# Gated delta rule in a two-layer decoder: the keys' scale in three instructions of VectorE instead of five of GpSimd, the queries' scale in two of GpSimd instead of five

## The chip, the cores and the metric

The kernel is one program on one core of a Trainium2 chip. The metric is the device time of one execution in microseconds (us). On the core, TensorE multiplies matrices into PSUM, VectorE (DVE in the profile) and ScalarE (ACT) work on elements, GpSimd (POOL) works on elements in SBUF, and SyncE (SP) issues most of the loads. Each engine runs its own instructions in order; they wait for each other by semaphores.

## The reference

Two decoder layers run over a prompt of 256 tokens and over 8 sequences of 4 sample tokens. The first layer's mixer is retention, the second's the gated delta rule; after each stands a gated ConvFFN. The change lies in the delta rule. What matters of it, cut:

```python
q = jnp.repeat(l2norm(q), rep, axis=2) * GDN_DK ** -0.5     # rep = 2 value heads for a key head
k = jnp.repeat(l2norm(k), rep, axis=2)
beta = jax.nn.sigmoid(b)
...
kb = kc * bc[..., None]                                      # keys times beta
L = jnp.where(tri_strict, jnp.einsum('bhid,bhjd->bhij', kb, kc) * decay, 0.0)
sol = lax.linalg.triangular_solve(eye + L, rhs, ...)         # (I + L)^-1
u, w = sol[..., :dv], sol[..., dv:]
v_new = u - w @ S
attn = jnp.einsum('bhid,bhjd->bhij', qc, kc) * decay
o = (qc * exp(G)) @ S + attn @ v_new
...
o = o * rsqrt(mean(o * o) + EPS) * norm_w * silu(z)
```

## The kernel before, in words

Activations are kept transposed: features on the 128 partitions, 288 columns of tokens (256 prompt, 32 sample). A projection is made by `product` (L527): for each output tile of 128 features 24 matmuls of 128 by 288, 8 for each of three pairs of high and low parts (`whi` with `hh`, `whi` with `hl`, `wlo` with `hh`), each weight block being split into `whi` by ScalarE (L416) and `wlo` by VectorE (L417) as it comes in.

The delta rule has 16 value heads in four groups of four heads (g is 0 to 3; two key heads in a group). `GDN_ORDER` (L34) gives the order of the projections: K is keys and queries (`gk`), V is values (`gv`), Z is the gate (`gz`), D is the output projection (`down`). Everything else is written as generators that are advanced every six matmuls, and so lies between the projections' matmuls. For each group:

- `gdn_norms` (L1157) sums the squares of keys and queries (tile `kss`, the last part by the small matmuls `pq`), takes the reciprocal root by nine small VectorE instructions (`rsqrt`, L541; the result is `krs`, its last instruction L557), and makes the keys' scale: `ksc[:,1]` is beta times the reciprocal norm squared, for two halves of the prompt (jt) and four heads; `ksc[:,0]` is its negative. This is where the first half of the change lies (L1190 to L1195).
- `gdn_scores` (L1275) multiplies keys by keys and queries (`pa`, 512 columns, and `pb`) for the group's two key heads, j is 0 and 1, and VectorE turns each pair into `gnn` and `gat` (L1291 to L1296: six instructions and two). `pa` and `pb` of the second key head take the PSUM banks of the first (`PA_TAGS`, L59), so they wait until its `gat` has been made.
- `gdn_inverse` (L1299) inverts I + L: first the 32 by 32 diagonal blocks by a chain of VectorE instructions (`mp`, `Ti`, L1332 to L1338, three a step), then a round trip through DRAM (`ud`, then `uc`, L1344 and L1346, both on SP's queue, which also carries the weights' loads `raw`), then small matmuls `pe` (L1358). The inverse of group g runs beside the norms of group g+1.
- `gdn_samples` (L1438) does the sample tokens (`psy`, `pso`); `gdn_heads` (L1562) and `gdn_finish` (L1607) solve, make the output, and update the state (`gpS`, L1636). `gdn_finish` makes the queries' scale `qs` (reciprocal norm times 1/sqrt(128), for eight columns of the prompt and one of the samples): the second half of the change (L1617 to L1622).

The program is handed to a scheduler which works out the order of each engine's instructions as the program is built. An engine's order is thus not always that of the code, and changes when instructions are changed.

Of the kernel before, what the change touches and what calls it, by code (L numbers as in the profile page):

```python
# [10 lines left out]
ALU = mybir.AluOpType  # L11
# [3 lines left out]
P = 128  # L15
# [280 lines left out]
class Program:  # L296
# [860 lines left out]
    def gdn_norms(self, g, d):  # L1157

        nc, gp = self.nc, self.gp
        t = lambda tag, shape, dt=F32, bufs=1: gp.tile(shape, dt, tag=tag, name=f"{tag}_{g}", bufs=bufs)  # L1160
        kqT, kt = d["kqT"], d["kt"]

        ss = t("kss", [P, 10], bufs=2)
        for j in range(2):
            yield from self.lag(d, ("kq", 0, j), CONV_STEPS)
            pt = self.aux(f"pk{g}{j}", "a")
            for i in range(2):
                nc.tensor.transpose(pt[:, i * P : (i + 1) * P], kqT[:, j, 0, i * P : (i + 1) * P], self.ident)
            for i in range(2):
                nc.scalar.activation(t("junk", [P, P], bufs=2), pt[:, i * P : (i + 1) * P], AF.Square, accum_out=ss[:, 2 * i + j : 2 * i + j + 1])  # L1170
            nc.scalar.copy(kt[:, :, j, :], pt[:, 0:TP].rearrange("p (i d) -> p i d", d=P))
        for j in range(2):
            yield from self.lag(d, ("kq", 1, j), CONV_STEPS)
            if j == 0:
                pq = self.aux(f"pq{g}", "a")
            for i in range(2):
                nc.tensor.matmul(pq[:, 2 * i + j : 2 * i + j + 1], lhsT=d["sq", j][:, i * P : (i + 1) * P], rhs=self.ones[:, 0:1], start=True, stop=True)
        while "sqd" not in d or self.nexg is None:
            yield
        for s in range(2):  # L1180
            nc.tensor.matmul(pq[:, 4 + s : 5 + s], lhsT=d["sqd"][:, s, :], rhs=self.ones[:, 0:1], start=True, stop=True)
        nc.vector.tensor_copy(ss[:, 4:10], pq[:, 0:6])
        nc.vector.tensor_scalar(ss, ss, EPS, None, ALU.add)
        rr = t("krs", [P, 10], bufs=2)
        self.rsqrt(rr, ss, 1.0, 0.0, f"k{g}")
        nm = t("knm", [P, 10], bufs=2)
        nc.vector.tensor_tensor(nm, ss, rr, ALU.mult)

        sc = t("ksc", [P, 3, 2, 4], bufs=2)
        for jt in range(2):  # L1190
            for j in range(2):
                bsl = self.beta[:, jt, 4 * g + 2 * j : 4 * g + 2 * j + 2]
                c = 2 * jt + j
                nc.gpsimd.tensor_scalar(sc[:, 1, jt, 2 * j : 2 * j + 2], bsl, rr[:, c : c + 1], rr[:, c : c + 1], ALU.mult, ALU.mult)
        nc.gpsimd.tensor_scalar(sc[:, 0], sc[:, 1], -1.0, None, ALU.mult)  # L1195
        d.update(sc=sc, rr=rr, nm=nm)

    def gdn_scores_all(self, ds):
# [408 lines left out]
    def gdn_finish(self, g, a):  # L1607

        nc, gp, A = self.nc, self.gp, self.A
        t = lambda tag, shape, dt=F32, bufs=1: gp.tile(shape, dt, tag=tag, name=f"{tag}_{g}", bufs=bufs)  # L1610
        big = lambda sh, dt=F32: self.big(sh, dt, "c", 512, BIG_C, 1)
        h4 = lambda v: v.rearrange("p (h d) -> p h d", d=P)
        kt, sc, rr, ss, osm, u, pos = (a[k] for k in ("kt", "sc", "rr", "ss", "osm", "u", "pos"))
# [2 lines left out]

        qs = t("qs", [P, 9], bufs=1)  # L1617
        f = float(P) ** -0.5
        for it in range(2):
            for j in range(2):  # L1620
                nc.gpsimd.tensor_scalar(qs[:, 4 * it + 2 * j : 4 * it + 2 * j + 2], self.ones[:, 0:2], rr[:, 4 + 2 * it + j : 5 + 2 * it + j], f, ALU.mult, ALU.mult)
        nc.gpsimd.tensor_scalar(qs[:, 8:9], rr[:, 9:10], f, None, ALU.mult)  # L1622
        s2 = t("oss2", [P, 9])
        nc.vector.tensor_tensor(s2, ss, qs, ALU.mult)
# [118 lines left out]
```

## Time and profile before

| | us |
|---|---|
| median of 3 runs | 1236.23 |
| lowest and highest | 1225.26, 1239.33 |
| the profiled execution's own time | 1233.65 |
| its span, from the first to the last instruction | 1231.9 |

TensorE is busy for 95% of the span, VectorE for 71%, ScalarE for 49%, GpSimd for 27%. TensorE's mean granted clock is 0.972 of full speed (2.4 GHz); where it isn't full it is half (1.2 GHz). The delta rule's part of the span reaches from about 600 to 960 us. An engine's idle time has a cost where TensorE, which is nearly always busy, is made to wait in the end. In the rows, a name in brackets says how long the engine had been idle before the instruction and what ended the wait.

### The profile page before, as it was taken

How to read it: one execution, taken by the hardware profiler on the slowest of the kernel's cores; microseconds unless marked ns; L12 is line 12 of the kernel's file. 1: busy time of each engine (PE TensorE's matmuls, PEld its weight loads, DVE VectorE, ACT ScalarE, POOL GpSimd, SP SyncE). 2: the span in 40 equal slices, each digit the busy share in tenths (PEclk: the TensorE clock that was granted, in tenths of full speed). 3: DMA queues.
4: the chain of work that ended last, by engine and by line, in shares of the span. 5: the costliest groups of instructions: out<-in, count | busy, mean ns of one | idle time of the engine just before them, and what ended most of it. 6: DMA issues, size and time to landing. Idle time of an engine off the chain costs nothing.

```text
span 1231.9 us, 24934 instructions
## 1 busy us (share of the span) xinstructions
PE 1164.1 (95%) x9486; PEld 1049.1 (85%) x9486; DVE 870.3 (71%) x2003; ACT 608.8 (49%) x1256; POOL 327.7 (27%) x507
## 2 busy tenths in 40 slices
PE   6999999999999999999989998988899899999996
PEld 2879798797969999997777788977889699999996
DVE  3657574765766666667679888797965588777775
ACT  2444534344445544444674645744544365555553
POOL 0213142251302122222252223233222113223232
PEclk9999999999999999999999988988989899999998
DMA  9998696877699556557636641533434897777621
GB/s 365 345 332 324 227 336 233 313 246 242 211 314 393 189 171 190 171 181 259 209 92 211 223 144 63 159 129 115 131 103 129 298 357 239 258 254 253 196 76 56
DMA packets 97480, 269.08 MB, mean 218 GB/s; under 512 B 26816, under 2 KB 29088, under 8 KB 97232
## 3 DMA queue, kind: packets, MB, share of 16 engines
q1 hardware_dynamic: 87456, 234.57, 57.2%
q0 software_dynamic: 8032, 29.16, 6.3%
q10 hardware_dynamic: 1872, 3.76, 0.8%
q8 instruction: 75, 1.23, 0.4%
q14 instruction: 45, 0.37, 0.1%
HBM read 236.06 MB, written 31.39 MB: 217 GB/s over the span
## 4 chain that ended last, share of the span: by engine, by line
PE 78%; DVE 12%; DMA 3%; ACT 3%; issue 2%; POOL 1%; SPq 0%; POOLq 0%; ACTq 0%; DVEq 0%
PE down L535 17%; PE fg L535 12%; PE fv L535 12%; PE pg L535 4%; PE pv L535 4%; PE adaP L455 4%; PE p L535 3%; PE gv L535 2%; PE gz L535 2%; DVE wlo L417 2%; DVE mp L1332 2%; PE gk L535 2%; PE pO L898 1%; PE pU L917 1%; PE pS L868 1%
## 5 line engine op out<-in xcount | busy, mean ns | idle before, releaser
L417 DVE TENSOR_TENSOR wlo<-more,whi 128x1024 fp32r<-128x1024 f32 x138 | 171.1, 1241 | 74.5 <-ACT whi L416 63.2
L416 ACT CAST whi<-more 128x1024 fp32r<-128x1024 f32 x138 | 144.3, 1047 | 136.5 <-PE down L535 53.1
L417 DVE TENSOR_TENSOR wlo<-raw,whi 128x1024 fp32r<-128x1024 f32 x123 | 155.4, 1267 | 70.6 <-ACT whi L416 48.4
L416 ACT CAST whi<-raw 128x1024 fp32r<-128x1024 f32 x123 | 128.1, 1044 | 133.5 <-PE down L535 32.8
L716 POOL TENSOR_TENSOR x<-x,dt 128x32 f32<-128x32 f32 x159 | 100.6, 634 | 135.2 <-DVE dt L714 134.1
L712 DVE SCALAR_TENSOR_TENSOR x<-down,mod,x 128x256 f32<-128x256 f32 x160 | 76.6, 479 | 51.3 <-PE down L535 50.5
L591 POOL TENSOR_TENSOR fal<-cv,fah 128x288 fp32r<-128x288 f32 x44 | 41.6, 945 | 215.7 <-ACT fah L590 180.7
L535 PE MATMUL down<-fal,whi 128*128 128x288 f32 x352 | 64.0, 294 | 0.0
L535 PE MATMUL down<-fah,whi 128*128 128x288 f32 x352 | 62.3, 294 | 0.0
L535 PE MATMUL down<-fah,wlo 128*128 128x288 f32 x352 | 62.1, 294 | 0.0
L535 PE MATMUL fg<-hh_ffn,whi 128*128 128x288 f32 x352 | 58.9, 300 | 1.2 <-ACT hh_ffn L637 1.2
L918 DVE SCALAR_TENSOR_TENSOR S<-S,pU 128x512 f32<-128x512 f32 x64 | 42.2, 684 | 24.2 <-PE pU L917 24.1
L535 PE MATMUL fv<-hh_ffn,whi 128*128 128x288 f32 x352 | 58.7, 298 | 0.0
L535 PEld LDWEIGHTS fg<-hh_ffn,whi 128*128 128x128 f32 x352 | 50.6, 189 | 5.6 <-ACT hh_ffn L646 2.6
L535 PE MATMUL fg<-hh_ffn,wlo 128*128 128x288 f32 x352 | 55.0, 296 | 0.0
L535 PE MATMUL fv<-hh_ffn,wlo 128*128 128x288 f32 x352 | 54.8, 295 | 0.0
L535 PE MATMUL fv<-hl_ffn,whi 128*128 128x288 f32 x352 | 54.3, 295 | 0.0
L535 PE MATMUL fg<-hl_ffn,whi 128*128 128x288 f32 x352 | 54.0, 295 | 0.0
L535 PEld LDWEIGHTS fv<-hh_ffn,whi 128*128 128x128 f32 x352 | 50.5, 189 | 2.5 <-ACT ftail L947 1.2
L535 PEld LDWEIGHTS down<-fah,whi 128*128 128x128 f32 x352 | 51.8, 188 | 0.8 <-ACT whi L416 0.4
L535 PEld LDWEIGHTS down<-fal,whi 128*128 128x128 f32 x352 | 52.3, 188 | 0.2 <-issue 0.2
L535 PEld LDWEIGHTS down<-fah,wlo 128*128 128x128 f32 x352 | 52.0, 188 | 0.0
(492 smaller groups left out, 2923.4 us busy)
## 6 DMA issues: line engine op xcount, KB each, us to landing
raw<-in_wada SPq DMA_DIRECT2D x69, 512.0 KB, 4.9
more<-in_wu SPq DMA_DIRECT2D x68, 512.0 KB, 4.9
raw<-in_wgi SPq DMA_DIRECT2D x48, 512.0 KB, 3.9
more<-in_wada SPq DMA_DIRECT2D x43, 512.0 KB, 5.9
more<-in_wd SPq DMA_DIRECT2D x41, 512.0 KB, 4.4
S<-in_sr SPq DMA_DIRECT2D x16, 1024.0 KB, 8.0
out_rs<-S POOLq DMA_DIRECT2D x16, 1024.0 KB, 8.1
raw<-in_wri SPq DMA_DIRECT2D x28, 512.0 KB, 4.9
```

Source lines behind the costliest of these rows:

```text
L416: nc.scalar.copy(hi[:, :c], r)
L417: nc.vector.tensor_tensor(lo[:, :c], r, hi[:, :c].bitcast(F32), ALU.subtract)
L455: nc.tensor.matmul(self.adaP[32 * g : 32 * g + 32, 0:256], lhsT=self.cs[:, k, :], rhs=rv[:, :, g, :], start=(k == 0), stop=(k == KT - 1), ...
L535: self.nc.tensor.matmul(out, lhsT=av[:, k, c0 : c0 + m], rhs=b[:, k, :], start=(k0 == 0 and i == 0), stop=(k1 == kts and i == len(seq) - 1))
L591: (nc.gpsimd if pool_lo else nc.vector).tensor_tensor(lo, src, hi.bitcast(F32), ALU.subtract)
L712: nc.vector.scalar_tensor_tensor(xm[:, :TP], p[:, :TP], g[:, 0:1], xm[:, :TP], ALU.mult, ALU.add)
L716: (nc.vector if gate == 11 and last and m == KT - 1 else nc.gpsimd).tensor_tensor(xv, xv, t, ALU.add)
L868: nc.tensor.matmul(pS, lhsT=kt[:, j, c * P : (c + 1) * P], rhs=vt[:, j, :], start=(j == 0), stop=(j == 1))
L898: nc.tensor.matmul(pO4[32 * g : 32 * g + 32, :], lhsT=qm[:, c, 4 * bb + g, :], rhs=S[bb, c][:, g, :], start=(bb == 0 and c == 0), stop=Fal ...
L917: nc.tensor.matmul(pU, lhsT=kms[g][:, c * P : (c + 1) * P], rhs=vst, start=True, stop=True)
L918: nc.vector.scalar_tensor_tensor(S[bb, c][:, g, :], S[bb, c][:, g, :], gamma4, pU, ALU.mult, ALU.add)
L1332: nc.vector.tensor_tensor(m, Ti[:, 0:k, :].rearrange("p j c -> p c j").unsqueeze(1).to_broadcast([P, w, 8, k]), X[:, 0:k, i:k].rearrange(" ...
```

## The change

The keys' scale: GpSimd made it by four instructions of 128 by 2 and one negation of 128 by 8. Now VectorE squares the four reciprocal norms into a new tile `kr2` (shown as `kr_0` to `kr_3` in the order), multiplies beta by it in one instruction whose second operand is repeated for the two heads, and negates the result. The queries' scale: four GpSimd instructions of 128 by 2 become one of 128 by 8; the fifth, for the samples, stays.

```diff
@@ gdn_norms
         sc = t("ksc", [P, 3, 2, 4], bufs=2)
-        for jt in range(2):
-            for j in range(2):
-                bsl = self.beta[:, jt, 4 * g + 2 * j : 4 * g + 2 * j + 2]
-                c = 2 * jt + j
-                nc.gpsimd.tensor_scalar(sc[:, 1, jt, 2 * j : 2 * j + 2], bsl, rr[:, c : c + 1], rr[:, c : c + 1], ALU.mult, ALU.mult)
-        nc.gpsimd.tensor_scalar(sc[:, 0], sc[:, 1], -1.0, None, ALU.mult)
+        r2 = t("kr2", [P, 4], bufs=2)
+        nc.vector.tensor_tensor(r2, rr[:, 0:4], rr[:, 0:4], ALU.mult)
+        by_h = lambda v: v.rearrange("p t (j h) -> p t j h", h=2)
+        nc.vector.tensor_tensor(
+            by_h(sc[:, 1]), by_h(self.beta[:, 0:2, 4 * g : 4 * g + 4]),
+            r2.rearrange("p (t j) -> p t j", j=2).unsqueeze(3).to_broadcast([P, 2, 2, 2]), ALU.mult
+        )
+        nc.vector.tensor_scalar(sc[:, 0], sc[:, 1], -1.0, None, ALU.mult)
         d.update(sc=sc, rr=rr, nm=nm)
@@ gdn_finish
-        for it in range(2):
-            for j in range(2):
-                nc.gpsimd.tensor_scalar(qs[:, 4 * it + 2 * j : 4 * it + 2 * j + 2], self.ones[:, 0:2], rr[:, 4 + 2 * it + j : 5 + 2 * it + j], f, ALU.mult, ALU.mult)
+        nc.gpsimd.tensor_scalar(qs[:, 0:8].rearrange("p (c h) -> p c h", h=2), rr[:, 4:8].unsqueeze(2).to_broadcast([P, 4, 2]), f, None, ALU.mult)
         nc.gpsimd.tensor_scalar(qs[:, 8:9], rr[:, 9:10], f, None, ALU.mult)
```

The number of matmuls, loads and ScalarE instructions is the same; GpSimd has 32 instructions fewer, VectorE 12 more. Up to the first group's scale all engines keep their order. Behind it the order moves in many places; three of them follow. The lines of the changed kernel are two higher from L1197 on.

VectorE at the first group's scale, before (`ssc` is the samples' scale):

```order
L557 SCALAR_TENSOR_TENSOR krs_7197<-rsu_k_7199,krs_7197 128x10
L1187 TENSOR_TENSOR knm_7209<-kss_6914,krs_7197 128x10
L1455 TENSOR_SCALAR ssc_7571<-bs,krs_7197 128x1
L1456 TENSOR_SCALAR ssc_7571<-ssc_7571 128x1
L1457 TENSOR_SCALAR ssc_7571<-ssc_7571,exs 128x1
L1291 SCALAR_TENSOR_TENSOR gnn_7225<-pa_7263,ksc_7211,gat_6973 128x128
```

The same place in the changed kernel:

```order
L557 SCALAR_TENSOR_TENSOR krs_7197<-rsu_k_7199,krs_7197 128x10
L1187 TENSOR_TENSOR knm_7209<-kss_6914,krs_7197 128x10
L1191 TENSOR_TENSOR kr_0_7212<-krs_7197 128x4
L1457 TENSOR_SCALAR ssc_7570<-bs,krs_7197 128x1
L1193 TENSOR_TENSOR ksc_7211<-beta,kr_0_7212 128x8
L1458 TENSOR_SCALAR ssc_7570<-ssc_7570 128x1
L1459 TENSOR_SCALAR ssc_7570<-ssc_7570,exs 128x1
L1197 TENSOR_SCALAR ksc_7211<-ksc_7211 128x8
L1293 SCALAR_TENSOR_TENSOR gnn_7224<-pa_7262,ksc_7211,gat_6973 128x128
```

The three new instructions stand between the samples' scale and the first `gnn`; TensorE's order is the same as before here.

VectorE at the second group's scale, before (`mp` and `Ti` belong to the first group's inverse):

```order
L557 SCALAR_TENSOR_TENSOR krs_7867<-rsu_k_7869,krs_7867 128x10
L1332 TENSOR_TENSOR mp_7389<-Ti_7332,X_7331 128x16x31
L1187 TENSOR_TENSOR knm_7879<-kss_7503,krs_7867 128x10
L1291 SCALAR_TENSOR_TENSOR gnn_7893<-pa_7933,ksc_7881,gat_7174 128x128
L1292 SCALAR_TENSOR_TENSOR gnn_7893<-pa_7933,gat_7174 128x128
```

The same place in the changed kernel:

```order
L557 SCALAR_TENSOR_TENSOR krs_7866<-rsu_k_7868,krs_7866 128x10
L1334 TENSOR_TENSOR mp_7388<-Ti_7331,X_7330 128x16x31
L1187 TENSOR_TENSOR knm_7878<-kss_7502,krs_7866 128x10
L1191 TENSOR_TENSOR kr_1_7881<-krs_7866 128x4
L1338 TENSOR_REDUCE Ti_7331<-mp_7388 128x16
L1193 TENSOR_TENSOR ksc_7880<-beta,kr_1_7881 128x8
L1340 SCALAR_TENSOR_TENSOR Ti_7331<-Ti_7331,xp_7338 128x8
L1197 TENSOR_SCALAR ksc_7880<-ksc_7880 128x8
L1334 TENSOR_TENSOR mp_7388<-Ti_7331,X_7330 128x256
L1293 SCALAR_TENSOR_TENSOR gnn_7891<-pa_7931,ksc_7880,gat_7174 128x128
```

Three instructions of the inverse have moved from behind the scores to ahead of them, between the new ones.

TensorE at the second group's second key head, before:

```order
L1493 MATMUL psy_7842<-t_0_7776,t_0_7592 128x128
L464 MATMUL adaT<-cst,adaev 128x128 x2
L1288 MATMUL pa_7967<-kqT_7484 128x512
L1493 MATMUL psy_7896<-t_0_7844,t_0_7592 128x128
L1289 MATMUL pb_7968<-kqT_7484 128x256
L535 MATMUL gz_8076<-hh_gdn,whi 128x288 x6
```

The same place in the changed kernel:

```order
L1495 MATMUL psy_7841<-t_0_7775,t_0_7591 128x128
L464 MATMUL adaT<-cst,adaev 128x128 x2
L1495 MATMUL psy_7894<-t_0_7843,t_0_7591 128x128
L535 MATMUL gz_8074<-hh_gdn,whi 128x288 x8
L535 MATMUL gz_8074<-hl_gdn,whi 128x288 x2
L1290 MATMUL pa_7965<-kqT_7483 128x512
```

Ten matmuls of the gate's projection have moved ahead of `pa`. In the third group seven have moved in the same way (twelve stand ahead of `pa` where five did), and on VectorE one `mp` and one `Ti` have moved ahead of the scores.

TensorE at the fourth group's second key head, before (`down` is the third group's output projection, of 96 matmuls; `pe` belongs to the third group's inverse):

```order
L535 MATMUL down<-gah_8870,whi 128x288 x4
L535 MATMUL down<-gal_8871,whi 128x288 x4
L535 MATMUL down<-gah_8870,wlo 128x288 x4
L1288 MATMUL pa_10053<-kqT_9421 128x512
L1289 MATMUL pb_10054<-kqT_9421 128x256
L1358 MATMUL pe_10121<-uc_10078,gnn_8993 32x32 x16
L535 MATMUL gv_10226<-hh_gdn,whi 128x288 x4
```

The same place in the changed kernel:

```order
L1290 MATMUL pa_10043<-kqT_9415 128x512
L1291 MATMUL pb_10044<-kqT_9415 128x256
L1360 MATMUL pe_10111<-uc_10068,gnn_8987 32x32 x16
L535 MATMUL down<-gah_8865,whi 128x288 x4
L535 MATMUL down<-gal_8866,whi 128x288 x4
L535 MATMUL down<-gah_8865,wlo 128x288 x4
```

Before, all 96 of `down` stood ahead of `pa`; now 72 do, and 24 stand behind the first `pe`. On VectorE the last `Ti` of the third group's inverse now stands only seven instructions ahead of this group's first `gnn`.

SP's queue at the same place, before:

```order
L1344 DMA ud_10073<-t1k_10071 32x256 x4
L402 DMA raw<-in_wgi 128x1024 x2
L1346 DMA uc_10078<-ud_10073 128x8x32
L1317 DMA Ti_10286<-in_unit 128x256
L402 DMA raw<-in_wgi 128x1024
```

The same place in the changed kernel:

```order
L1346 DMA ud_10063<-t1k_10061 32x256 x4
L1319 DMA Ti_10276<-in_unit 128x256
L1348 DMA uc_10068<-ud_10063 128x8x32
L402 DMA raw<-in_wgi 128x1024 x3
```

The way back from DRAM (`uc`) now stands ahead of the two weight loads that it stood behind.

## Rows read from the trace of the kernel before

**Rows 1.** The page: the span, and the engines' busy time with its share of the span and their instructions.

```profile
span 1231.9 us, 24934 instructions
PE 1164.1 (95%) x9486; PEld 1049.1 (85%) x9486; DVE 870.3 (71%) x2003; ACT 608.8 (49%) x1256; POOL 327.7 (27%) x507
```

**Rows 2.** The waits of TensorE from 580 to 960 us, what it was to issue and what it waited for: us in total, times, the longest.

```profile
PE pa L1288 <- DVE gat L1295: 7.3, 4, 2.2
PE gpS L1636 <- DVE bigc L1631: 5.8, 3, 4.3
...
PE psy L1493 <- ACT t L1488: 2.6, 2, 2.4
```

**Rows 3.** The tiles of the keys' scale and of the queries' scale: the instructions that write them, with the shortest, median and longest duration in ns, and the first and last start.

```profile
L1194 POOL TENSOR_SCALAR ksc<-beta,krs x16: 327/335/1374, 624.2 to 841.7; 128x2 f32<-128x2 f32 x16
L1195 POOL TENSOR_SCALAR ksc<-ksc x4: 242/250/252, 627.2 to 842.1; 128x8 f32<-128x8 f32 x4
L1621 POOL TENSOR_SCALAR qs<-ones,krs x16: 258/268/977, 625.6 to 894.1; 128x2 f32<-128x2 f32 x16
```

**Rows 4.** The timeline at the first group's scale: start, duration, engine, line, instruction; in brackets the idle time before it and what ended it.

```profile
622.98 1.05 POOL L1245 TENSOR_TENSOR decay<-cst_g,ghl 128x512 fp32r<-128x512 f32 x1 [1.38 <-PE pd L1262]
623.16 0.90 DVE L557 SCALAR_TENSOR_TENSOR krs<-rsu_k,krs 128x10 f32<-128x10 f32 x1
624.10 0.17 DVE L1187 TENSOR_TENSOR knm<-kss,krs 128x10 f32<-128x10 f32 x1
...
627.24 0.25 POOL L1195 TENSOR_SCALAR ksc<-ksc 128x8 f32<-128x8 f32 x1
627.40 0.55 PE L535 MATMUL gv<-hl_gdn,whi 128*128 128x288 f32 x3
...
627.53 0.35 DVE L1291 SCALAR_TENSOR_TENSOR gnn<-pa,ksc,gat 128x128 f32<-128x128 f32 x1 [2.77 <-POOL ksc L1195]
...
628.97 0.68 DVE L1295 TENSOR_TENSOR gat<-pa,gat 128x512 f32<-128x512 f32 x1
...
629.70 0.70 PE L1288 MATMUL pa<-kqT 128*128 128x512 f32 x1 [1.75 <-DVE gat L1295]
```

**Rows 5.** The timeline at the second group's scale.

```profile
678.04 0.16 DVE L557 SCALAR_TENSOR_TENSOR krs<-rsu_k,krs 128x10 f32<-128x10 f32 x1
678.16 1.14 DVE L1332 TENSOR_TENSOR mp<-Ti,X 128x496 f32<-128x496 f32 x1
...
680.85 0.35 DVE L1291 SCALAR_TENSOR_TENSOR gnn<-pa,ksc,gat 128x128 f32<-128x128 f32 x1 [1.47 <-POOL ksc L1195]
681.10 0.38 PE L464 MATMUL adaT<-cst,adaev 128*128 128x128 f32 x2
...
683.02 1.13 PE L1288 MATMUL pa<-kqT 128*128 128x512 f32 x2 [1.54 <-DVE gat L1295]
...
683.42 0.66 DVE L1336 TENSOR_REDUCE Ti<-mp 128x16 f32<-128x496 f32 x1
```

**Rows 6.** The timeline at the third group's scale.

```profile
760.47 0.16 DVE L557 SCALAR_TENSOR_TENSOR krs<-rsu_k,krs 128x10 f32<-128x10 f32 x1
...
762.06 0.82 PE L535 MATMUL gz<-hh_gdn,whi 128*128 128x288 f32 x5
...
762.45 0.35 DVE L1291 SCALAR_TENSOR_TENSOR gnn<-pa,ksc,gat 128x128 f32<-128x128 f32 x1 [1.38 <-POOL ksc L1195]
...
764.72 1.10 PE L1288 MATMUL pa<-kqT 128*128 128x512 f32 x2 [1.84 <-DVE gat L1295]
764.82 0.62 DVE L1332 TENSOR_TENSOR mp<-Ti,X 128x256 f32<-128x256 f32 x1
```

**Rows 7.** The timeline at the fourth group's scale (SPq is SP's queue).

```profile
834.56 0.41 DVE L1336 TENSOR_REDUCE Ti<-mp 128x8 f32<-128x256 f32 x1
...
838.50 2.77 SPq L402 DMA_DIRECT2D raw<-in_wgi  x2
...
841.48 1.26 SPq L1346 DMA_DIRECT2D uc<-ud  x1
...
842.37 0.35 DVE L1291 SCALAR_TENSOR_TENSOR gnn<-pa,ksc,gat 128x128 f32<-128x128 f32 x1 [1.47 <-POOL ksc L1195]
...
844.54 1.33 PE L1288 MATMUL pa<-kqT 128*128 128x512 f32 x2 [2.19 <-DVE gat L1295]
...
846.21 1.22 PE L1289 MATMUL pb<-kqT 128*128 128x256 f32 x2 [0.34 <-DVE gat L1296]
846.32 0.83 POOL L1353 COPY TT<-uc 32x256 f32<-32x256 f32 x2 [3.78 <-DMA uc<-ud]
...
849.60 0.63 PE L1358 MATMUL pe<-uc,gnn 32*32 32x32 f32 x15 [2.18 <-DVE uc L1347]
```

**Rows 8.** The engines' busy time in stretches of the span: us, then busy time (and instructions) of PE, PEld, DVE, ACT, POOL, then TensorE's granted clock, the DMA share and GB/s.

```profile
844.00:848.00 4.00, 2.55 (x4) 0.80 (x4) 3.40 (x10) 0.85 (x3) 0.79 (x2) 0.67 0.36 88
848.00:852.00 4.00, 2.40 (x45) 2.06 (x47) 3.82 (x11) 1.13 (x3) 1.81 (x3) 0.50 0.00 0
852.00:856.00 4.00, 4.00 (x64) 3.74 (x61) 1.66 (x6) 1.97 (x5) 1.22 (x4) 0.55 0.38 137
```

**Rows 9.** The same view, for a stretch between a scale and the next state update, and for the stretch of that update.

```profile
700.00:720.00 20.00, 19.82 (x259) 18.20 (x258) 13.26 (x36) 16.99 (x57) 5.90 (x16) 1.00 0.57 153
720.00:740.00 20.00, 17.02 (x172) 14.64 (x172) 19.22 (x60) 6.32 (x22) 6.72 (x12) 0.83 0.48 157
```

## The prediction

> **What bounds the kernel now.** I read the page first: TensorE is busy for 1164 of 1232 us [rows 1], so a change is worth what it gives TensorE to do earlier, and not what it takes from VectorE or GpSimd. Then TensorE's waits in the delta rule's part [rows 2]: the longest in total, 7.3 us in four waits, is `pa` waiting for `gat`, once a group. Who is late there is in the timeline of each of the four places. In each, the last instruction of `krs` ends, GpSimd makes `ksc`, VectorE stands idle for 1.38 to 2.77 us until GpSimd's negation (L1195) is done, then makes six `gnn` and one `gat`, and TensorE issues `pa` within 0.1 us of that `gat`'s end, after an idle time of 1.75, 1.54, 1.84 and 2.19 us [rows 4 to 7]. So the keys' scale lies on the path that ends last, four times, and the sum is made of these four places. From the first `gnn` to the end of `gat` takes 2.12 us (627.53 to 629.65), of which the six `gnn` take 0.24 us each [rows 4].
>
> The sum is made against the profiled execution: 1233.65 us, 1.75 us more than its span. The median of the runs shown is 2.6 us above it, so a time on the median's scale has 2.6 us added.
>
> **The new instructions.** Not one of their forms is in the trace. The nearest rows are VectorE's small instructions on the same tiles, 0.16 to 0.17 us, and at the upper end `krs` at the first group, 0.90 us [rows 4, 5]. I take 0.17 us, because the long one ran beside a GpSimd instruction (the third rival below) and the others didn't: three are 0.5 us for a group, where GpSimd needed four of 0.335 and one of 0.25 us, 1.6 us [rows 3]. They are added to VectorE's queue and end no wait by being there, so they can't gain by themselves; the bounds of a group's three are 0.5 and 2.7 us.
>
> **First group, 1.75 us.** Now `krs` ends at 624.06 and the first `gnn` starts at 627.53, because GpSimd also had the queries' scale ahead of the negation. In the changed order seven small instructions stand between; each starts as soon as the one ahead, at most 0.17 us on, so `gnn` starts by about 625.2 and `gat` ends by 627.3. TensorE's order is unchanged here, and its work ahead of `pa` ends at 627.95 (627.40 and 0.55) [rows 4]. The whole wait goes, 1.75 us; the next limit is TensorE's own work, 0.65 us behind.
>
> **Second group, 0.7 us.** Here the new order gives VectorE three instructions of the inverse before the scores. From 679.30, when `mp` ends: `kr`, `Ti` (0.66), `ksc`, `Ti`, the negation, `mp` (0.6): about 1.6 us, and `gnn` starts at 680.9, as late as now (680.85) [rows 5]. What changes is what TensorE does meanwhile. A matmul of a projection takes 0.135 us (five take 0.82, three 0.55) [rows 4, 6], and the ten that were moved ahead of `pa` are 1.35 us. They stand behind the second `psy`, which needs a VectorE instruction that now comes behind four `gnn`, so it can start at about 682.3. TensorE is then idle from 681.48 to 682.3 in place of 1.54 us, and `pa` finds its `gat` made: 0.7 us won. The inverse's three instructions fill VectorE's idle time, and are done some 3 us earlier.
>
> **Third group, 1.15 us.** One `mp` and one `Ti` move ahead of the scores, about 0.6 and 0.4 us [rows 6, 7]; `gnn` starts at about 762.2 in place of 762.45, and `gat` ends at 764.4. Seven more matmuls stand ahead of `pa`, 0.95 us, so TensorE's work reaches to 763.7 or so where it ended at 762.88. The wait of 1.84 falls to 0.7 us [rows 6].
>
> **Fourth group, from +0.2 to -3.1 us, taken at -0.6 us.** This is the place where the order moves most, and it is not clearly a gain. Now TensorE waits 2.19 us at `pa`, 0.34 at `pb` and 2.18 at `pe`, 4.7 us together [rows 7]. In the new order the norms' last matmuls stand 21 projections' matmuls earlier, and I reckon with 0 to 0.5 us at `pa`. But `pe` needs `uc`, the third group's way through DRAM, and the last `Ti` that it starts from now stands some 1.3 us ahead of the first `gnn`. Now, from the end of that `Ti` (834.97) to `uc`'s landing (846.32) pass 11.3 us, of which 2.8 are the two weight loads ahead of it on SP's queue [rows 7]; they are behind it in the new order, so 8.5 to 11.3 us. With the transpose `pe` can start 9.0 to 11.8 us after that `Ti`. TensorE is there 1.3 (to `gnn`), 2.1 (to `gat`'s end) and 1.1 us (`pa` and `pb`) after it, 4.5 us. So it waits 4.5 to 7.3 us at `pe` where it waited 2.5 in `pb` and `pe`, with at most half a microsecond at `pa`: from 0.2 us better to 3.1 worse. I take 0.6 us worse, near the better end, because the queue's order is known.
>
> **What costs or gives nothing.** The queries' scale takes about 0.8 us less of GpSimd for a group [rows 3]; its reader on VectorE comes long after it and TensorE's list of waits has no entry that it ends [rows 2]. VectorE gets 12 times 0.17, 2.0 us more work; between a scale and the next state update it has room for it (13.26 us of 20 busy, rows 9). If that cover is gone, the 2.0 us are paid in full.
>
> **Sum.** 1.75 + 0.7 + 1.15 - 0.6 = 3.0 us: 1233.65 - 3.0 = 1230.6, and on the median's scale **1233 us**.
>
> **Rivals.**
>
> *The gain grows.* At the fourth group the granted clock falls to about half behind the waits: TensorE's 2.55, 2.40 and 4.00 us of work from 844 to 856 at 0.67, 0.50 and 0.55 cost 3.8 us over full speed [rows 8]. With the waits cut differently the stretch could go. And the inverse's chain is some 3 us ahead of now at the second and third group; if the waits at `gpS` and `psy`, which end on VectorE's work behind that chain (5.8 and 2.6 us, rows 2), halve with it, that is 4.2 us. 3.0 + 3.8 + 4.2 = 11: 1222.7, median's scale 1225. For it: VectorE is the one that is late there. Against it: `pe` still makes TensorE wait for several microseconds at the fourth group.
>
> *VectorE becomes the bound, and it is slower.* Place: the state updates, as from 720 to 740 us, where VectorE is busy for 19.22 of 20 us and TensorE for 17.02 [rows 9]. What TensorE wins at the scores it then waits at `gpS`, and VectorE's 2.0 us more and the fourth group's 0.6 us remain: 1236.2, median's scale 1239. It decides if VectorE has no idle time left from a scale to the next update. For it: the nearly full row. Against it: the 20 us ahead of that row leave it 6.7 us idle.
>
> *The new instructions wait for GpSimd.* At the first group `krs`, whose two inputs lie in SBUF, took 0.90 us beside GpSimd's `decay` (622.98 to 624.03), and ended with it; alone it takes 0.16 [rows 4, 5]. `kr` and `ksc` are of that kind. If both lose 0.74 us in all four groups, that is 5.9 us, less the 0.65 us of slack at the first and a quarter of a microsecond at the second: 5.0, so 1235.7, median's scale 1238. Against it: at the second and third group GpSimd stands idle before `ksc` now, and at the first only the queries' scale is due. The Trainium skill (SBUF — State Buffer, section "Who interferes with whom") has it as a rule: a VectorE instruction with two SBUF inputs and a GpSimd instruction that reads SBUF shut each other out for a whole instruction, whoever comes first. The trace agrees at `krs`, and the same rule speaks for the change too: GpSimd's longest `ksc` took 1.37 in place of 0.335 us [rows 3]. By the rule alone the change would lie between the sum's gain of 3.0 us and this rival's loss of 2.0.
>
> **How the numbers follow.** The forecast has a chance of 0.54, the larger gain 0.14, VectorE as the bound 0.24, the wait for GpSimd 0.08. On the median's scale they stand at 1233, 1225, 1239 and 1238. The runs shown spread from 11 us below their median to 3 above, and a median of three moves by some 2 or 3 us for that alone. The range that leaves out no more than 2 in 10 takes in the three upper cases with that spread and half of the larger gain: 1223 to 1241. Within 1%, 12.4 us, is about what a measurement of this kernel can't tell from no change: only the far half of the larger gain lies below 1223.9, and with what I don't see faster has 0.10; beyond 1248.6 no case reaches, and I keep 0.06 for an order that does worse than its pieces; the same has 0.84.
>
> **What would show it.** In the changed trace: the idle time before the first `gnn` of each group, now 2.77, 1.47, 1.38 and 1.47 us behind GpSimd, should be gone; `pa`'s four waits should fall from 7.3 to about 2 us; `pe`'s wait at the fourth group should grow to some 4 or 5 us. `kr` and `ksc` at 0.17 us show the new instructions' price, and anything near 0.9 the third rival. If `gpS` waits longer by what `pa` waits less, it is the second. The forecast is wrong in kind if the clock's stretches of half speed come at other places than now, because each costs as much as the whole sum.

## The result

The changed kernel takes 1223.12 us, the median of 20 executions, against 1232.34 us for 20 of the kernel before: a ratio of 0.9925, with a 95% interval of 0.991 to 0.994. That is 9.2 us (7.4 to 11.1) where 3.0 were forecast. It is within 1%, and inside the range by 0.1 us; the direction was right and the size three times too small.

The page after, the lines that answer to [rows 1]:

```profile
span 1221.1 us, 24926 instructions
PE 1156.2 (95%) x9486; PEld 1042.6 (85%) x9486; DVE 872.4 (71%) x2015; ACT 608.5 (50%) x1256; POOL 315.8 (26%) x475
```

TensorE has as many matmuls as before and is busy for 7.9 us less with them: they ran faster, which is the clock. GpSimd gave up 11.9 us and VectorE took on 2.1.

TensorE's waits after, from 580 to 960 us, which answer to [rows 2]:

```profile
PE gpS L1636 <- DVE bigc L1631: 4.0, 2, 3.1
PE pe L1360 <- DVE uc L1349: 3.7, 2, 2.6
PE gpS L1636 <- DVE Ti L1340: 3.7, 1, 3.7
...
PE psy L1495 <- ACT t L1490: 2.0, 2, 1.8
...
PE psy L1495 <- DVE t L1497: 1.5, 3, 0.9
...
PE pa L1290 <- DVE gat L1297: 0.6, 1, 0.6
```

`pa`'s four waits of 7.3 us are down to one of 0.6. Some of it is given back: `gpS` waits for 7.7 us where it waited for 5.8, `pe` for 3.7 where it was 2.5, and `psy` for 3.5 where it was 2.6, together 4.0 us.

The new instructions in the views of their tiles (shortest, median and longest in ns), which answer to [rows 3]:

```profile
L1191 DVE TENSOR_TENSOR kr<-krs x4: 147/162/178, 625.0 to 827.6; 128x4 f32<-128x4 f32 x4
...
L1193 DVE TENSOR_TENSOR ksc<-beta,kr x4: 151/160/167, 625.3 to 827.8; 128x8 f32<-128x8 f32 x4
...
L1197 DVE TENSOR_SCALAR ksc<-ksc x4: 159/161/168, 625.6 to 828.3; 128x8 f32<-128x8 f32 x4
```

The timeline after, at the first group's scale, which answers to [rows 4]:

```profile
623.77 1.05 POOL L1247 TENSOR_TENSOR decay<-cst_g,ghl 128x512 fp32r<-128x512 f32 x1 [1.38 <-PE pd L1264]
623.95 0.91 DVE L557 SCALAR_TENSOR_TENSOR krs<-rsu_k,krs 128x10 f32<-128x10 f32 x1
...
624.95 0.26 POOL L1621 TENSOR_SCALAR qs<-krs 128x8 f32<-128x8 f32 x1
624.97 0.18 DVE L1191 TENSOR_TENSOR kr<-krs 128x4 f32<-128x4 f32 x1
...
625.84 0.35 DVE L1293 SCALAR_TENSOR_TENSOR gnn<-pa,ksc,gat 128x128 f32<-128x128 f32 x1
...
627.27 0.68 DVE L1297 TENSOR_TENSOR gat<-pa,gat 128x512 f32<-128x512 f32 x1
...
628.85 1.02 PE L1290 MATMUL pa<-kqT 128*128 128x512 f32 x2
```

From the end of `krs` (624.86) to the first `gnn` are 0.98 us, where there were 3.47. `gat` ends at 627.95, 0.9 us ahead of `pa`, and TensorE doesn't wait. And at the fourth group, which answers to [rows 7]:

```profile
827.24 0.41 DVE L1338 TENSOR_REDUCE Ti<-mp 128x8 f32<-128x256 f32 x1
...
828.58 0.35 DVE L1293 SCALAR_TENSOR_TENSOR gnn<-pa,ksc,gat 128x128 f32<-128x128 f32 x1
...
831.31 1.02 PE L1290 MATMUL pa<-kqT 128*128 128x512 f32 x2
832.17 0.59 PE L1291 MATMUL pb<-kqT 128*128 128x256 f32 x2
...
832.44 0.38 SPq L1348 DMA_DIRECT2D uc<-ud  x1
...
835.00 0.83 POOL L1355 COPY TT<-uc 32x256 f32<-32x256 f32 x2 [6.11 <-DMA uc<-ud]
```

**Where the time came from in the two profiles.** The whole gain lies between the first group's first `pb` and the end of the last `gz`; behind it both kernels need 276 us. This is that stretch, first before, then after: us, then busy time of PE, PEld, DVE, ACT, POOL, then TensorE's granted clock.

```profile
622.63:956.03 333.40, 303.05 (x2808) 273.06 (x2809) 263.94 (x694) 180.25 (x470) 98.36 (x190) 0.94 0.46 138
```

```profile
623.42:945.34 321.92, 294.92 (x2808) 266.82 (x2809) 266.82 (x706) 180.13 (x470) 86.94 (x158) 0.97 0.48 142
```

It is 11.5 us shorter. TensorE's idle time in it (length less PE's busy time) falls from 30.35 to 27.00 us: 3.4 us, and 3.0 were forecast. The other 8.1 us are the same 2808 matmuls at a mean clock of 0.97 in place of 0.94.

**Where it came from over all executions.** A profile shows one execution, and the mean clock of the whole program is on record for each. For the kernel before it went from 0.968 to 0.984 in the 104 executions of the comparisons below, on four chips: mean 0.9756, mean time 1232.1 us (between 1231.7 and 1232.4 for each chip). For the changed kernel it was 0.9797 and 1223.3 us in 19 executions. Executions that were disturbed are left out of all means: one of the changed kernel, two of the kernel before and one of the second group alone. The profiled execution of before, at 0.972, was well below its kernel's mean; that of after, at 0.979, was within 0.001 of it. So the pair of profiles overstates the clock's part: 0.007 between them, 0.0041 between the means. Within one kernel, an execution with 0.001 more clock is 0.63 us shorter (252 executions of the 14 kernels, each set against its own kernel's means; correlation -0.72). If all of TensorE's speed were passed on it would be 1.2 us, a thousandth of the span. By these two slopes, an estimate, the clock gave 2.5 to 4.9 us of the 8.8 between the means, and 3.9 to 6.2 us are left at equal clock.

### The profile page after: what moved, and what is told of

Its sections match the earlier page's. It is cut to its first block, busy times and chain, and to the rows that moved or that the text cites. A ratio compares the mean times of both kernels' runs of the same rounds, so it can differ in the third digit from the quotient of the medians.

```text
span 1221.1 us, 24926 instructions
## 1 busy us (share of the span) xinstructions
PE 1156.2 (95%) x9486; PEld 1042.6 (85%) x9486; DVE 872.4 (71%) x2015; ACT 608.5 (50%) x1256; POOL 315.8 (26%) x475
## 4 chain that ended last, share of the span: by engine, by line
PE 79%; DVE 12%; DMA 4%; ACT 3%; issue 2%; POOL 1%; SPq 0%; POOLq 0%; ACTq 0%; DVEq 0%
PE down L535 17%; PE fg L535 12%; PE fv L535 12%; PE pg L535 4%; PE pv L535 4%; PE adaP L455 4%; PE gv L535 4%; PE p L535 3%; DVE mp L1334 2%; PE gk L535 2%; PE gz L535 2%; DVE wlo L417 2%; PE pO L898 1%; PE pU L917 1%; DVE Ti L1338 1%
```

## The experiments

All kernels are compared with the kernel before on the same chip. The expectations were written with the two profiles in hand, and so speak of 8 us for the clock; the paragraph above came later. The table has the readings; the wait is VectorE's, for the scale ahead of the first `gnn` of the groups, idle is TensorE's in the stretch above, both from one profile; time and clock are means over all executions. The standard error of a kernel's difference from the kernel before is 0.5 to 1.2 us in time and 0.0006 to 0.0013 in clock, so that single differences in clock of 0.001 to 0.002 are not clear of noise.

| kernel | wait, us | idle, us | time, us | clock | ratio (95% interval) |
|---|---|---|---|---|---|
| scale twice | 13.4 | 34.4 | 1241.0 | 0.9718 | 1.0072 (1.0046 to 1.0099) |
| before | 7.1 | 30.4 | 1232.1 | 0.9756 | |
| spare VectorE work | 6.6 | 32.2 | 1230.9 | 0.9778 | 0.9991 (0.9971 to 1.0011) |
| queries' scale only | 6.0 | 31.9 | 1232.5 | 0.9748 | 1.0009 (0.9987 to 1.0031) |
| keys, group 2 only | 5.7 | 28.5 | 1227.9 | 0.9779 | 0.9967 (0.9943 to 0.9991) |
| keys, group 3 only | 5.6 | 28.7 | 1225.7 | 0.9795 | 0.9952 (0.9933 to 0.9970) |
| keys, group 4 only | 5.6 | 29.2 | 1227.8 | 0.9778 | 0.9965 (0.9947 to 0.9983) |
| keys, group 1 only | 4.3 | 28.4 | 1229.3 | 0.9772 | 0.9985 (0.9962 to 1.0008) |
| three on GpSimd | 2.5 | 28.1 | 1228.1 | 0.9765 | 0.9973 (0.9955 to 0.9992) |
| nine on VectorE | 0 | 26.0 | 1226.5 | 0.9775 | 0.9962 (0.9942 to 0.9982) |
| keys' scale only | 0 | 25.5 | 1223.7 | 0.9792 | 0.9947 (0.9929 to 0.9965) |
| whole change | 0 | 27.0 | 1223.3 | 0.9797 | 0.9925 (0.9910 to 0.9940) |
| negated scale first | 0 | 28.1 | 1222.7 | 0.9840 | 0.9937 (0.9914 to 0.9961) |
| one wait filled | 7.3 | 30.4 | 1229.8 | 0.9797 | 0.9984 (0.9967 to 1.0002) |

**The keys' scale alone.** The first half of the diff; the queries' scale stays five instructions.

> Only the keys' scale goes to VectorE; the queries' scale stays five GpSimd instructions. Every engine but GpSimd has the same order of work as with the whole change. Theory (the gain is about 3 us of TensorE's waits and about 8 us of matmuls that run at the full instead of the half clock, and both follow from the keys' scale): the whole gain stays, ratio to the kernel before 0.991 to 0.994. Rival (part of the gain is GpSimd's relief: 12 instructions of 0.335 us in all): the gain is smaller by 1 to 4 us, ratio 0.995 to 0.997.

0.9947 (0.9929 to 0.9965), between the theory's band (to 0.994) and the rival's (from 0.995): the interval takes in parts of both, and by itself the run doesn't decide. The wait is gone and the mean time is 0.4 us from the whole change's. It doesn't show GpSimd's relief to give anything, and the next run says so more directly.

**The queries' scale alone.** The second half of the diff.

> Only the queries' scale is shortened; the keys' scale is as before, and all engines but GpSimd keep the order of the kernel before. Theory: nothing waits for these instructions, so no change, ratio 0.999 to 1.001. Rival (GpSimd's relief): 1 to 4 us faster, ratio 0.997 to 0.999.

1.0009 (0.9987 to 1.0031): no change, as the theory had it. With the order of all engines but GpSimd kept, 12 instructions less of GpSimd are worth nothing here.

**The first group alone.**

```
-        for jt in range(2):
...
+        if g == 0:
+            (the three VectorE instructions)
+        else:
+            (the five GpSimd instructions)
```

> The keys' scale goes to VectorE for the first group alone; TensorE, ScalarE and SyncE keep the order of the kernel before, and VectorE has three instructions more. Theory (the first term of the sum): the wait of 1.75 us of pa at the first group goes and nothing else changes, ratio 0.9982 to 0.9990, and all of TensorE's later work is 1.5 to 2 us earlier. Rival (the stretches at the half clock move with any shift): the gain differs from 1.75 us by 2 us or more in either direction, and the granted clock between 700 and 960 us differs from that of the kernel before.

0.9985 (0.9962 to 1.0008), 1.8 us by its middle, which is the 1.75 us of the forecast, though the interval takes in zero. In its profile TensorE's idle time is 1.9 us less than before. But that execution was at a clock of 0.972 and a span of 1234.0 us, 2.1 us above that of before: a single pair of profiles can't time an edit of this size. The order of TensorE's instructions is that of the kernel before, so here the wait is shortened with the order held.

**Three instructions, all on GpSimd.** The change with `nc.gpsimd` for the three.

> The whole change, but the three new instructions of the keys' scale run on GpSimd: three instead of five there, at some 0.34 to 0.5 us each. Theory (the length of the chain up to the first gnn counts, and the engine only through it): about 0.3 to 0.7 us less of the scale's 1.7 us at each group, so 0.5 to 2 us of waits less, and of the clock's part anything from none to half: ratio 0.995 to 0.9995. Rival (fewer and wider instructions, or the order that the scheduler makes of them, give the gain, whatever the engine): ratio 0.991 to 0.994.

0.9973 (0.9955 to 0.9992): between the two, inside the theory's band. GpSimd's product took 0.21 and its negation 0.24 us at the median, VectorE still waited for 2.5 us in all, and the gain is less than half. So fewer instructions help where they shorten the wait. That the engine counts for the rest fits, but isn't shown alone, since the order is another one too.

**The second, the third and the fourth group alone.** The diff is that of the first group, with `g == 1`, `g == 2` and `g == 3`.

> The keys' scale goes to VectorE for the second group alone. Theory of the sum (only the wait of the first pa of the group counts): 0.7 us faster, ratio 0.9994. Theory of the clock (a wait that goes also moves the stretches at the half clock behind it): the wait goes, and the matmuls of gpS for the second group and the projections around it, which ran at the half clock from 733 to 741 us, run at the full one: 2 to 4 us faster, ratio 0.997 to 0.9985.

> The keys' scale goes to VectorE for the third group alone. Theory of the sum: 1.15 us faster, ratio 0.9991. Theory of the clock: the stretch between the third group's first pa and the samples' psy, which was 3.3 us shorter with the whole change than before, is 2 to 4 us shorter here too; with the wait 3 to 5 us faster, ratio 0.996 to 0.9975. Rival (it is the order that the scheduler makes that counts, since VectorE's and TensorE's order move here by far more than in the other single groups): the gain shows at other places than behind the third group's pa, or is a loss.

> The keys' scale goes to VectorE for the fourth group alone. Theory of the sum (the wait of pa goes, but the triangular inverse of the third group is then late and pe waits for uc): 0.6 us slower, between 0.2 us faster and 3.1 us slower, ratio 1.0005 (0.9998 to 1.0025). Theory of the clock (with the whole change this stretch became 4.4 us shorter, with pe waiting 2.6 us): 3 to 5 us faster, ratio 0.996 to 0.9975. Rival (the 4.4 us there came from what the first three groups had moved, not from the fourth group's scale): within 1 us of the kernel before.

They gained 4.1, 5.9 and 4.3 us by the middles of the intervals, where the sum had 0.7, 1.15 and a loss of 0.6. The fourth group's scale alone makes the kernel faster; the sign of that term was wrong. And the four single groups don't add up: their ratios fall short of one by 1.3% together, 16 us, and the whole change gains 9. In part this is the clock, which is won once: against 0.9756 it rises by 0.0015, 0.0023, 0.0038 and 0.0022 in the four, 0.0098 together, and by 0.0041 with all of them. At full passing on (1.2 us for 0.001) the clock explains 1.8, 2.7, 4.6 and 2.6 us of the single gains in mean time (2.8, 4.2, 6.4, 4.3); 1.0, 1.5, 1.8 and 1.7 us are left, 5.9 together, against 3.9 for the whole change. With the smaller slope the remainders sum to 11.5 against 6.2. So the clock explains a part of the excess, and not all of it.

The third group's rival, the order, fits as well. Read in order of their starts, with like neighbours merged, TensorE's instructions differ from the kernel before in 0, 5, 44 and 7 places with the first to the fourth group alone; from the whole change the third group alone differs in only 9. It brings nearly the whole new order with it. And 3.9 us of the 9.3 by which the stretch above is shorter in its profile lie between the fourth group's last `gk` and its `gv` (821 to 857 us before), where the scale is still GpSimd's and TensorE's wait at `pa` is even longer (2.19 us before):

```profile
833.71 1.33 PE L1298 MATMUL pa<-kqT 128*128 128x512 f32 x2 [3.45 <-DVE gat L1305]
```

How much of its gain is order, and how much wait, no run separates.

**Nine instructions on VectorE.** `for _ in range(3):` around the three.

> The whole change, with the three new VectorE instructions issued three times over: six more of 0.15 to 0.16 us in each group, 24 in all. Theory (VectorE's time counts only where TensorE waits behind it): 0.95 us later at each of the four groups' first gnn, so 1 to 4 us slower than the whole change, ratio to the kernel before 0.994 to 0.998. Rival (VectorE is the bound, all of its time is on the path): 3.8 us and more over the whole change. Rival (the order counts more than the durations): any value outside 0.992 to 0.999.

0.9962 (0.9942 to 0.9982). By the mean times it is 3.2 us behind the whole change for 24 instructions of 0.16 us, 3.8 us. If that is their price, VectorE's time on this path is paid for nearly in full, as at the four places where the wait was; but TensorE's order also differs from that of the whole change, in 55 places, and the runs don't tell 0.95 us a group on the path from VectorE as a bound altogether.

**Another order, nothing shortened.** GpSimd's five instructions stay, and behind them stand

```
...
+        k2 = t("kb2", [P, 2, 2, 4], bufs=1)
+        nc.vector.tensor_tensor(r2, rr[:, 0:4], rr[:, 0:4], ALU.mult)
...
+        nc.vector.tensor_scalar(k2[:, 0], k2[:, 1], -1.0, None, ALU.mult)
```

> The kernel before, with GpSimd's five instructions for the keys' scale as they are, and three instructions like the change's on VectorE besides, into tiles that nobody reads. Nothing that the change shortens is shorter here, and VectorE has 12 instructions of 0.15 to 0.16 us more; but the scheduler makes another order of it (TensorE's differs from the kernel before in about as many places as with the whole change). Theory (the gain behind the 3 us of waits follows from the shorter scale): no gain, 0 to 2 us slower, ratio 1.000 to 1.002. Rival (the order of the kernel before was an unlucky one for the clock, and nearly any other gives half-clock time back): 3 to 6 us faster, ratio 0.995 to 0.9975, with TensorE's waits as long as before and less time at the half clock.

0.9991 (0.9971 to 1.0011): no gain to be measured. Its stretch is as long as that of before, with more idle time and a little less of the half clock:

```profile
622.70:957.01 334.31, 302.11 (x2809) 272.83 (x2809) 264.91 (x707) 180.22 (x470) 97.80 (x190) 0.95 0.45 138
```

So it is not enough that the scheduler makes another order. This was the rival that the single groups had made likely; one other order doesn't rule out every one, but it takes away the reason to believe that any other would do. The clock, at 0.9778, is 0.0021 above that of before (twice the standard error) although nothing was shortened, as much as with the second or the fourth group alone: so what those two win in clock needn't come from the shorter scale.

**The negated scale first.** `by_r` is the squared norm, repeated for the two heads.

```
-        nc.vector.tensor_tensor(by_h(sc[:, 1]), ...)
-        nc.vector.tensor_scalar(sc[:, 0], sc[:, 1], -1.0, None, ALU.mult)
+        nc.vector.scalar_tensor_tensor(by_h(sc[:, 0]), by_h(self.beta[...]), -1.0, by_r, ALU.mult, ALU.mult)
+        nc.gpsimd.tensor_scalar(sc[:, 1], sc[:, 0], -1.0, None, ALU.mult)
```

> The whole change in another form: VectorE squares the reciprocal norms and makes the negated scale, which gnn reads, in one instruction; GpSimd makes the positive one from it afterwards, which is read only tens of us later. One VectorE instruction of 0.16 us less ahead of each first gnn. Theory of the path: 0 to 0.7 us faster than the whole change, ratio to the kernel before 0.991 to 0.9935. Rival (the order that the scheduler makes of it decides): anything between 0.988 and 0.998.

0.9937 (0.9914 to 0.9961), not to be told from the whole change. Its clock is the highest of all (0.9840, six executions) and yet its time is lower by only 0.6 us: what it has in clock over the whole change, 0.0043 or 2.7 us and more by the slopes above, is lost elsewhere. The 1.1 us more of idle time in its profile are a part of that; the rest is open.

**Filling one wait.** Ahead of the second group's first `psy`, in the kernel before:

```
+            if g == 1 and n == 0:
+                idle = self.aux("idle", "s")
+                for _ in range(6):
+                    nc.tensor.matmul(idle[:, 0:P], lhsT=self.ident, rhs=self.ident, start=True, stop=True)
```

> The kernel before, with six extra matmuls of 128 by 128 ahead of the samples' first psy of the second group; one lies earlier in TensorE's order, five (about 1.1 us) in the wait of 2.4 us ahead of that psy, behind which the clock was at the half level from 733 to 740 us. Their result is read by nobody. Theory (the clock falls because TensorE stands idle there): with the wait half filled, the granted clock stays at 1.00 from 730 to 742 us and the eight matmuls of the second gpS take about 2.0 us, not 3.75. Rival (the fall has another reason): 0.5 to 0.7 there as in the kernel before, and 3.5 us or more for those matmuls. The order behind 745 us changes, so the whole time tells little: ratio 0.995 to 1.001.

The timeline there (`idle` are the extra matmuls):

```profile
733.40 1.27 PE L1495 MATMUL idle<-cst 128*128 128x128 f32 x10
736.93 0.49 PE L1497 MATMUL psy<-t,t 128*128 128x128 f32 x2 [2.25 <-ACT t L1488]
...
739.42 3.38 PE L1640 MATMUL gpS<-bigc,kn 128*128 128x256 f32 x8 [1.86 <-DVE bigc L1635]
```

The run doesn't decide it: the work ahead reached this place later, the extra matmuls ran before the wait, and 2.25 us of it are still there, with 1.86 more at `gpS`. `gpS` ran at the half clock for most of its time (3.38 us, where the changed kernel's eight took 1.97 at the full one). That the clock falls behind idle time is neither shown nor refuted by it. Over ten executions its mean clock is that of the whole change (0.9797), and its mean time is 6.5 us longer, of which the extra matmuls themselves are some 1.3: a higher clock alone doesn't make the gain.

**The opposite of the change.** `for _ in range(2):` around GpSimd's five instructions.

> The kernel before, with GpSimd's five instructions for the keys' scale issued twice over: some 1.6 to 1.7 us more ahead of the first gnn of every group (four of 0.335 us and one of 0.25 us), the opposite of the change. Theory (the time from the reciprocal norms to the first gnn counts through TensorE's waits and through the clock behind them): VectorE waits 12 to 14 us for the scale rather than 7.1, TensorE's idle time between the first group's first pb and the last gz grows by 3 to 6 us from 30.4, and the time at the half clock does not fall below the 38 us of the kernel before: 4 to 10 us slower, ratio 1.003 to 1.008. Rival (the kernel before stands at an unlucky point, and any change of the scale's length moves away from it): no slower, ratio 0.996 to 1.001, with half-clock time down to 20 to 28 us, as in all the kernels with a shorter scale.

1.0072 (1.0046 to 1.0099), 8.9 us slower and inside the theory's band. The wait of VectorE, in the kernel before, with the spare work, with three instructions on GpSimd, and in this one:

```profile
DVE gnn L1291 <- POOL ksc L1195: 7.1, 4, 2.8
```

```profile
DVE gnn L1300 <- POOL ksc L1195: 6.6, 4, 2.6
```

```profile
DVE gnn L1293 <- POOL ksc L1197: 2.5, 4, 0.9
```

```profile
DVE gnn L1292 <- POOL ksc L1196: 13.4, 4, 4.5
```

And the stretch:

```profile
622.82:960.93 338.11, 303.71 (x2808) 274.60 (x2809) 263.99 (x693) 179.68 (x470) 104.33 (x210) 0.94 0.45 136
```

TensorE's idle time is 4.0 us above that of before. So 6.3 us more of the wait cost 8.9 us, and 7.1 us less of it gain 8.8: about 1.2 to 1.4 us for each, in both directions, with another clock both times (0.9718, 0.9756 and 0.9797).

This kernel's order is not that of the kernel before either: TensorE's differs in 41 places. But three runs have nearly one order, 4 to 12 places from each other and 39 to 41 from the kernel before: three on GpSimd, the spare work and this one. Their waits are 2.5, 6.6 and 13.4 us, and their mean times 1228.1, 1230.9 and 1241.0. With the order nearly held, a longer wait costs time, and that the length of the scale counts is shown; its price was 0.7 us for each us over the first step and 1.5 over the second. That the order has no part in the gain is not shown: from the third group alone to the whole change, 9 places apart, 5.6 us of wait are worth only 2.4 us.

## Why the prediction was right, and what was too small

**The path and the new instructions: right.** VectorE no longer waits for the scale. `kr` and the two `ksc` take 0.16 us, the 0.17 that was taken; the bounds of up to 0.9 were not needed. The queries' scale at nothing was right.

**The range: held by luck.** The kernel before had a median of 1232.3 us in 20 executions where the three that were seen had 1236.2, and the gain was 6.2 us above the sum. Both moved the time down, and only the part of the range that was kept for the larger gain, at a chance of 0.14, took it in, by 0.1 us.

**First group, 1.75 us: right.** The wait is gone. Measured from the first `pb`, `pa` starts 1.64 us sooner (623.42 to 628.85, before 622.63 to 629.70), and that group alone gained 1.8 us. **Third group, a wait of 0.7 us left: right**, 0.59 in the trace, and the one that is left. **Second group:** no wait for `gat` is left at `pa` here either.

**Fourth group: wrong in sign.** `pa` waits for nothing, as the better bound had it. The failed term is `uc`'s way, taken at 8.5 to 11.3 us from the last `Ti`: it landed 7.35 us behind it (827.65 to 835.00). SP issued it 4.79 us after that `Ti`, where it was 6.51, since the weight loads were behind it now, and that I had counted; but from issue to use it took 2.56 us, where it was 4.84 [rows 7], and that I had left as it was. `pe` waited for 2.6 us and not for 4.5 to 7.3. What made the transfer faster wasn't tried.

**The clock: the term that the sum didn't have.** The sum came to 3.0 us of TensorE's idle time, and the two profiles show 3.4. That they are so near is luck: the fourth group gave 2.1 us (4.7 of waits before, 2.6 after) where 0.6 were to be lost, and waits that the sum had at nothing took as much back, 1.9 us at `gpS` and 0.8 at another group's `pe`. And the sum held the time of the matmuls themselves fixed. Between the profiles they became 8.1 us shorter; between the means the clock is worth 2.5 to 4.9 us. The larger gain had a stretch at half the clock in it, but only at the fourth group, for 3.8 us and at a chance of 0.14 (one slice of 4 us at 0.57, from 836 to 840 us, is left there of the three [rows 8]), and its other half failed: the waits at `gpS` and `psy` were not halved, they grew. That rival's 1225 us is nearer to the 1223 measured than the forecast of 1233, for a reason of which half was true. The half clock shows at other places than before, which the prediction had named as the sign that it is wrong in kind. Here are three slices around the second group's `gpS`, and the first `psy` and `gpS` there, before and after (the last line is the slice that is left at the fourth group):

```profile
728.00:732.00 4.00, 2.28 (x17) 2.05 (x17) 4.00 (x12) 0.38 (x1) 1.07 (x1) 1.00 0.54 189
732.00:736.00 4.00, 2.86 (x7) 2.23 (x8) 4.00 (x12) 0.63 (x2) 1.72 (x5) 0.59 0.43 131
736.00:740.00 4.00, 4.00 (x18) 3.61 (x17) 3.36 (x12) 2.04 (x6) 0.62 (x1) 0.56 0.02 4
...
732.67 0.80 PE L1493 MATMUL psy<-t,t 128*128 128x128 f32 x2 [2.39 <-ACT t L1488]
...
734.18 3.75 PE L1636 MATMUL gpS<-bigc,kn 128*128 128x256 f32 x8 [0.47 <-DVE bigc L1631]
```

```profile
728.00:732.00 4.00, 1.56 (x11) 1.12 (x9) 4.00 (x10) 0.62 (x2) 1.39 (x3) 1.00 0.64 210
732.00:736.00 4.00, 3.74 (x24) 3.40 (x25) 4.00 (x12) 1.74 (x4) 0.58 (x1) 1.00 0.12 45
736.00:740.00 4.00, 3.11 (x24) 2.66 (x23) 4.00 (x9) 2.66 (x13) 2.64 (x4) 1.00 0.17 66
...
730.74 0.49 PE L1495 MATMUL psy<-t,t 128*128 128x128 f32 x2 [1.80 <-ACT t L1490]
...
732.26 1.97 PE L1636 MATMUL gpS<-bigc,kn 128*128 128x256 f32 x8 [0.90 <-DVE bigc L1631]
...
836.00:840.00 4.00, 4.00 (x67) 3.64 (x62) 2.63 (x9) 0.86 (x3) 1.92 (x4) 0.57 0.37 115
```

Before, TensorE stood idle for 2.39 us ahead of `psy` and the clock went to half; after, for 1.80 us, and it stayed. But with the keys' scale alone, which has the same order on TensorE and VectorE as the whole change, the same place fell to half behind 1.92 us of idle time:

```profile
732.00:736.00 4.00, 4.00 (x13) 3.37 (x12) 4.00 (x13) 0.86 (x3) 0.00 (x0) 0.50 0.00 0
736.00:740.00 4.00, 4.00 (x31) 4.00 (x30) 2.36 (x7) 3.59 (x13) 2.69 (x4) 0.81 0.19 70
...
729.82 0.49 PE L1495 MATMUL psy<-t,t 128*128 128x128 f32 x2 [1.92 <-ACT t L1490]
...
731.35 3.75 PE L1638 MATMUL gpS<-bigc,kn 128*128 128x256 f32 x8 [0.91 <-DVE bigc L1633]
```

So a stretch at half the clock can't be assigned to a place from one profile; what the change moved is the mean clock over many executions, from 0.9756 to 0.9797. That the shorter wait is what moved it is not shown: with the spare work and with the one wait filled, where VectorE's wait was about as long as before (6.6 and 7.3 us), it rose by 0.0021 and 0.0041.

**VectorE as the bound: half right.** The full row of its place stayed full: VectorE is busy for 19.86 of 20 us from 720 to 740 us after, 19.22 before [rows 9], and `gpS`, `psy` and `pe` wait longer. It didn't decide, because those waits gave back only part of `pa`'s. **The new instructions waiting for GpSimd: fell.** They took 0.147 to 0.178 us, and at eight of the twelve GpSimd did nothing at the time. At the first group it did: `kr`, with its inputs in SBUF, ran from 624.97 to 625.15 inside GpSimd's `qs` (624.95 to 625.21), which reads SBUF too, and took 0.178 us. `krs` there, beside `decay`, still takes 0.91 us. The rule that such a pair shut each other out for a whole instruction (the Trainium skill, SBUF — State Buffer, "Who interferes with whom") agrees with `krs` and doesn't show at `kr`; GpSimd's times in a profile are rough, so that one row doesn't refute it.

**What stays open:** why one shortened group alone already wins 0.0015 to 0.0038 of the whole change's 0.0041 in clock, and whether a removed wait or the new order does it; and how much of the clock's speed reaches the end, between 0.63 and 1.2 us for 0.001.

## What to carry to other kernels

A wait of one engine for a chain of tiny instructions on another can cost more than the idle time that TensorE shows behind it: over the whole change and over its opposite 1.2 to 1.4 us for each us of the wait, and the clock was another one both times. It is no rate to reckon with: between pairs of kernels with nearly one order it was 0.4 to 3 (the last from the second and the fourth group alone, 4.2 and 4.3 us for 1.4 and 1.5 us of the wait). Before a sum is made from a profile, look at the mean clock of its execution against that of others; 0.001 of it is 0.6 to 1.2 us in this kernel, as much as the smaller edits. And where an edit changes the scheduler's order, run a kernel that has a new order and nothing shortened, and one that makes the suspected wait longer, and count in the traces how far their orders are apart: what two kernels of nearly one order show of the wait is not open to the order as a rival.

## What was not expected of the hardware

Executions of one kernel, the kernel before on four chips, differ in TensorE's mean granted clock from 0.968 to 0.984 (on each single chip from 0.968 or 0.969 to 0.980 or more), and in time with it (0.63 us for 0.001; correlation -0.72 over all kernels, -0.77 in the kernel before); that is over half of the variance of its times. GpSimd's product of two inputs of 128 by 8, one of them repeated, took 0.21 us at the median, less than one of the four instructions of 128 by 2 that it replaced (0.335 us), and VectorE's took 0.16.
